# The last matrix product of a hybrid mLSTM and attention block: its buffers, its look-ahead, its sums and its weight pieces laid out anew

## The chip, the cores and the metric

The kernel runs on one core of a Trainium2 chip. The metric is the device time of one execution in microseconds (us), as the median of several runs. All arithmetic is on float32 data.

## The reference, cut to what matters

One block works on 1024 tokens with 16 meta tokens ahead of them, width 1024. The change lies in the end of it, and in the layout of four of its weights:

```python
mix = g_a * (y_a @ w_branch_a) + g_b * (y_b @ w_branch_b)
h = h + mix @ w_out
z = rms_norm(h, norm2_g) @ w_ff1
h = h + jnp.square(jax.nn.relu(z)) @ w_ff2
return h[:, N_META:]
```

`w_ff1` is 1024 x 4096 and `w_ff2` 4096 x 1024. In the kernel `w_branch_a` is `w_a`.

## The kernel before, in words

**Products.** A float32 operand is split into a high part (a copy in TensorE's fp32r type) and a low part (the operand minus its high part), and each product is three matmuls: high by high, low by high, high by low (`mm3`). The four large products named above also use a 2 x 2 block scheme with seven block products in place of eight (numbered 1 to 7); the price is sums of operand blocks beforehand and sums of results behind. A tile is 128 x 1024 float32 (4 KB per partition).

**The last stages, in the order of TensorE.** `cols_a` (four column pairs of `w_a`), `out_p` (`w_out`), `cols_1` (sixteen column pairs of `w_ff1`, w10 to w115; the squared relu of each goes to DRAM as `z2d`), and then `rows_2`, the last stage, which is `z2d` times `w_ff2`. `rows_2` is four groups f0 to f3 (`NG`), each a quarter of the inner dimension. A group has 14 products: seven block products in two halves, q = 0 and q = 1. In names, f1w16l is group 1, weight side, q = 1, block product 6, low part; z is the other side.

**What a group of the last stage does.** `quarters2` loads four z tiles (zr) and four weight tiles (w2r) for each q through SP's queue: 16 tiles a group. `parts` (class `Rows`, from L1240) splits them for products 1 and 2 as they are, then makes eight sums (s1, t1, and six in place) for each q, and splits their results for products 6, 7, 5, 4, 3. A split is a copy on ACT (`SC.copy` in `hilo`, L1086) and a subtraction (`rest`, L233) into two new tiles. So a group has 28 splits and 16 sums, of 128 x 1024 each. `mul` issues 24 matmuls of 512 columns for a product; behind the second half of a block product four PSUM banks (128 x 512 each, six banks in the pool `psx`) are added to that block product's accumulator (`out_2`, L1482): on ACT as plain copies for four of the seven in group 0, on DVE otherwise. In the last group `out_2` also adds accumulators to each other and sends 16 pieces to the output (L1510).

**Who does a sum.** `either` (L230) gives each sum and each remainder to DVE or to POOL, whichever by a kept account would be done first; the third argument makes POOL dearer. `share_gp` sets it (L1576): in the last stage it is `BULK` = 3.0.

**Order.** The list `seq` holds all products. Before product n is issued, `ensure(n + ah, n)` prepares products up to n + ah; `ah` is `AH2` = 2 in the last stage, so each product's splits and sums are written two products ahead. The loads of the next group's two halves are hooked 5 and 2 products ahead of its first (L1571). A scheduler orders each engine's instructions from this.

**Buffers.** Pool `slots` has 44 tiles (`NSLOT`, L27); loads, split parts and, in the last stage, all 14 accumulator tiles live there. Pool `late` has tag "r" with 7 tiles (`late`, L1072; s1 and t1 come from it) and tag "wr" with 3 for the pieces of `w_a` and `w_ff1` (`raw`, L1161).

**Weight pieces.** A piece of `w_a` and `w_ff1` is read as 128 x 8 x 128 out of the row-major matrix, 512 bytes at a time; a piece of `w_out` and `w_ff2` as 128 x 2 x 512, 2 KB at a time.

Of the kernel before, what the change touches and what calls it, by code (L numbers as in the profile page):

```python
# [17 lines left out]
S = 1024  # L18
# [21 lines left out]
KB, FF = 2, 9  # L40
D2 = 2
NP_ = 2
AH1, AH2, NE1, NE2, ZH, BULK = 5, 2, 1, 5, 11, 3.0
TCARGS = dict(schedule_with_timeline_sim=True)

C_G1, C_G2, C_CW, C_CB, C_NG, C_SK, C_GQ, C_GK, C_GB, NCOL = 0, 8, 16, 40, 48, 56, 64, 65, 66, 67
# [136 lines left out]
def build(tc, A, taps=None):  # L183
# [18 lines left out]
    def slot(name, dt=F32):  # L202
        return sp.tile([128, L], dt, name=name, tag="S")
# [949 lines left out]
    class Cols:  # L1153


        def __init__(self, name, src, z, out, raw_slot):
            self.name, self.src, self.z, self.out, self.raw_slot = name, src, z, out, raw_slot
            self.r, self.c, self.t = {}, {}, {}
            self.gen = self.parts()

        def raw(self, e):  # L1161
            if e not in self.r:
                n = f"{self.name}r{e}"
                t = slot(n) if self.raw_slot else LP.tile([128, 1024], F32, name=n, tag="wr", bufs=3)
                dma(t[:, 0:1024].rearrange("p (k c) -> p k c", k=8),
                    self.src[:, e * 128:e * 128 + 128].rearrange("(k p) c -> p k c", p=128))
                self.r[e] = t
            return self.r[e]

        def part(self, i, src):  # L1170
            c = late("c", F32R) if (self.name, i) in LATE_C else slot(f"{self.name}c{i}", F32R)
            SC.copy(c[:, 0:512], src)
            rest(c[:, 512:1024], src, c[:, 0:512], share_gp[0])
            self.c[i] = c
# [65 lines left out]
    class Rows:  # L1240


        def __init__(self, name, quarters, out):
            self.name, self.quarters, self.out = name, quarters, out
            self.q, self.z, self.w = {}, {}, {}
            self.gen = {}

# [1 line left out]
            if q not in self.q:  # L1249
                self.q[q] = self.quarters(q)  # L1250

        def part(self, q, i, a, b):
            self.z[q, i] = hilo(a, f"{self.name}z{q}{i}")
            self.w[q, i] = hilo(b, f"{self.name}w{q}{i}")

        def parts(self, q):
            self.load(q)
            c = slice(0, 1024)
            (a11, a12, a21, a22), (b11, b12, b21, b22) = [[t[:, c] for t in x] for x in self.q[q]]
            self.q[q] = None  # L1260
# [12 lines left out]
            sub(b21, b21, b11)
            for i, a, b in ((6, a11, b11), (7, a21, b12), (5, s1, t1), (4, a22, b21), (3, a12, b22)):
                self.part(q, i, a, b)
                yield

        def prep(self, i, q):
# [44 lines left out]
            V.scalar_tensor_tensor(g, b, 2.0, g, OP.mult, OP.add)  # L1323
        return out

    cols_a = [Cols(f"wa{p}", A["w_a"][:, p * 256:p * 256 + 256], za, out_a(p), False) for p in range(4)]
    sy = s_parts(yq, za, "y")
    NBS = ((0, 512), (512, 512))
    load_gb(0)
# [43 lines left out]
                SC.activation(o, pt, AF.Copy, scale=col(C_G2 + k))  # L1373

    def out_quarters(q):
        a = [ga[p, h_] for p, h_ in ((q, 0), (2 + q, 0), (q, 1), (2 + q, 1))]
        b = []
        for kh in range(2):
            for ch in range(2):
                t = slot(f"wo{q}{kh}{ch}")  # L1380
                r0 = kh * 512 + q * 256
                dma(t[:, 0:1024].rearrange("p (a c) -> p a c", a=2),
                    A["w_out"][r0:r0 + 256, ch * 512:ch * 512 + 512].rearrange("(a p) c -> p a c", p=128))
                b.append(t)
        return a, b

    def load_x2(t):
# [136 lines left out]
    def hook(d, n, fn):  # L1524
        d.setdefault(n, []).append(fn)
# [2 lines left out]
    n_o = len(seq)  # L1528
    seq += [(out_p, i, q) for i in (1, 2, 6, 5, 3, 7, 4) for q in range(2)]
    n_1 = len(seq)  # L1530
    group(cols_1, NE2)
    n_2 = len(seq)
    seq += [(o, i, q) for o in rows_2 for i in (1, 2, 6, 7, 5, 4, 3) for q in range(2)]

# [33 lines left out]
        hook(before, n - 7 if p >= NE2 else max(n - 5, n_1 + 2 * NE2), lambda p=p: (cols_1[p].raw(0), cols_1[p].raw(1)))  # L1568
    for g in range(1, NG):
        for q in range(2):  # L1570
            hook(before, n_2 + 14 * g - 5 + 3 * q, lambda g=g, q=q: rows_2[g].load(q))  # L1571

    for n, (o, i, q) in enumerate(seq):
        for fn in before.get(n, ()):
            fn()
        share_gp[0] = BULK if n >= n_1 + 2 * NE2 + 14 else 1.5 if n<n_o else 1.5 if n<n_1 else 1.0  # L1576
        ah = AH2 if n >= n_2 or n_o <= n < n_1 - 6 else AH1
        if n_1 <= n < n_1 + 2 * NE2:
            ah = n_1 + 2 * NE2 - 1 - n
        ensure(n + ah, n)  # L1580
        o.mul(i, q)
# [3 lines left out]
def layout(inp):  # L1585
# [16 lines left out]
    out["wk"] = f("mlstm_wk")
    out["mbias"] = f("na_meta_bias")
# [46 lines left out]
```

## Time and profile before

| | us |
|---|---|
| median of 3 runs | 1702.43 (1701.75 to 1706.6) |
| the profiled execution | 1708.2 |
| its span, first to last instruction | 1706.4 |
| TensorE (PE) busy | 1613.5 (95%) |
| VectorE (DVE) busy | 1237.2 (73%) |
| ScalarE (ACT) busy | 784.8 (46%) |
| GpSimd (POOL) busy | 525.9 (31%) |
| mean granted TensorE clock | 0.982 |
| last stage, from its first matmul to the end of the span | 1361.34 to 1706.40 |

The span is of one execution under the profiler, 5.8 us above the median of the plain runs in its own time; 1.8 us of that execution lie outside the span. Busy times are sums over an engine's instructions; matmuls are pipelined, so their recorded durations overlap, and the pace is read from their starts. The granted clock is a share of TensorE's full speed (1.00 is 2.4 GHz, 0.50 is 1.2 GHz).

### The profile page before, as it was taken

To read this page: it belongs to the slowest core of one execution; us is meant where nothing else is said; L and a number is where in the kernel's file an instruction comes from. 1 tells how busy PE (TensorE), PEld (TensorE's weight loads), DVE (VectorE), ACT (ScalarE), POOL (GpSimd) and SP (SyncE) were. 2 spreads that over 40 slices of the span, in tenths; PEclk is the share of its full clock that TensorE was granted. 3 is DMA by queue.
4 is the path that set the end of the run, shared out by engine and by line. 5 is a ranking of instruction groups with operands and counts; after the bars stand their busy time and mean duration, and the time that the engine had idled before them with its cause. 6 is when DMAs were issued, how large, how long until landed. Compare 5 with 4: busy or idle time off the path is not lost. (4 is left out here: it accounts for less than half of the span.)

```text
span 1706.4 us, 22334 instructions
## 1 busy us (share of the span) xinstructions
PE 1613.5 (95%) x8009; PEld 1361.6 (80%) x8009; DVE 1237.2 (73%) x2121; ACT 784.8 (46%) x1398; POOL 525.9 (31%) x509
## 2 busy tenths in 40 slices
PE   5999799999999999999899898899999989999998
PEld 4988789988989988888677676688888868777776
DVE  4438657574767686872689989786667787988897
ACT  6367666666747676752322444222222334333230
POOL 4110212122242222213567666610000042323274
PEclk9999999999999999999999899999999999999999
DMA  6352744546363443438547031143222735132311
GB/s 194 63 131 63 184 116 117 131 112 149 75 172 83 106 96 79 104 82 259 176 133 246 25 99 62 37 160 112 99 99 100 257 107 190 60 138 83 115 50 74
DMA packets 114190, 202.18 MB, mean 118 GB/s; under 512 B 10760, under 2 KB 62344, under 8 KB 114080
## 3 DMA queue, kind: packets, MB, share of 16 engines
q1 hardware_dynamic: 95648, 137.71, 24.3%
q0 software_dynamic: 18432, 63.05, 17.1%
q8 instruction: 63, 1.03, 0.2%
q14 instruction: 47, 0.39, 0.1%
HBM read 153.44 MB, written 38.76 MB: 113 GB/s over the span
## 5 line engine op out<-in xcount | busy, mean ns | idle before, releaser
L137 PE MATMUL g<-xh,wl 128*128 128x512 f32 (+3 forms) x832 | 304.2, 366 | 10.1 <-DMA wl<-w_in 10.1
L137 PE MATMUL g<-xh,wh 128*128 128x512 f32 (+3 forms) x832 | 306.2, 368 | 5.4 <-DVE xm L137 2.7
L137 PE MATMUL g<-xl,wh 128*128 128x512 f32 (+3 forms) x832 | 302.6, 364 | 0.0
L137 PEld LDWEIGHTS g<-xh,wl 128*128 128x128 f32 x832 | 158.1, 190 | 29.6 <-DMA wl<-w_in 11.5
L137 PEld LDWEIGHTS g<-xh,wh 128*128 128x128 f32 x832 | 158.5, 191 | 24.2 <-DVE xm L137 3.0
L137 PEld LDWEIGHTS g<-xl,wh 128*128 128x128 f32 x832 | 158.5, 190 | 16.8
L174 POOL DMA_DIRECT2D wl<-w_in x44 | 40.5, 922 | 166.5 <-ACT wl L137 74.6
L137 DVE TENSOR_TENSOR acc<-acc,pf 128x512 f32<-128x512 f32 x96 | 63.0, 677 | 9.8 <-PE pf L137 9.8
L137 DVE CUSTOM_DVE_ANT_0 P<-ps,bt 128x400 f32<-128x400 f32 x64 | 36.0, 570 | 45.4 <-PE pp L137 21.6
L137 ACT ACTIVATE wl<-wh 128x1024 fp32r<-128x1024 f32 (+1 forms) x52 | 51.5, 991 | 25.1 <-PE g L137 11.7
L137 ACT COPY pu<-pf 128x512 f32<-128x512 f32 x20 | 11.7, 585 | 108.1 <-PE pf L137 108.1
L137 DVE SCALAR_TENSOR_TENSOR C<-C,decb,pu 128x258 f32<-128x258 f32 x52 | 23.4, 480 | 33.9 <-PE pu L137 33.5
L137 ACT ACTIVATE P<-P,mn 128x400 f32<-128x400 f32 x64 | 40.3, 630 | 15.2 <-DVE mn L137 14.7
L137 DVE SCALAR_TENSOR_TENSOR zq<-zq 128x512 f32<-128x512 f32 x64 | 46.2, 721 | 0.7
L137 POOL COPY bt<-mbias 128x32 f32<-128x32 f32 x32 | 8.3, 262 | 115.7 <-DVE mn L137 115.6
L161 POOL DMA_DIRECT2D wh<-w_in x44 | 29.4, 668 | 37.4 <-ACT plo L137 10.2
L137 DVE TENSOR_TENSOR zq<-pf,pu 128x512 f32<-128x512 f32 x32 | 21.9, 686 | 24.9 <-PE pf L137 24.9
L137 DVE TENSOR_SCALAR P<-P,sm 128x384 f32<-128x384 f32 (+1 forms) x128 | 38.5, 364 | 0.9
L137 DVE TENSOR_TENSOR zq<-pf,sp 128x512 f32<-128x512 f32 x32 | 22.0, 687 | 23.6 <-PE pf L137 23.4
L137 DVE TENSOR_TENSOR ptl<-pp,pth 128x384 fp32r<-128x384 f32 x64 | 35.5, 555 | 2.7 <-ACT pth L137 2.0
L137 DVE TENSOR_TENSOR pu<-pf,pu 128x512 f32<-128x512 f32 x40 | 27.3, 683 | 12.9 <-PE pf L137 12.9
L137 ACT CAST pth<-pp 128x512 fp32r<-128x512 f32 x60 | 34.0, 581 | 5.4 <-PE pp L137 5.2
(2379 smaller groups left out, 5040.3 us busy)
## 6 DMA issues: line engine op xcount, KB each, us to landing
wh<-w_in POOLq DMA_DIRECT2D x44, 512.0 KB, 5.3
wl<-w_in POOLq DMA_DIRECT2D x44, 512.0 KB, 5.7
z2d<-zq SPq DMA_DIRECT2D x32, 512.0 KB, 4.4
zr<-z2d SPq DMA_DIRECT2D x32, 512.0 KB, 4.0
w2r<-w_ff SPq DMA_DIRECT2D x32, 512.0 KB, 8.3
bt<-rpbd SPq DMA_DIRECT2D x256, 32.0 KB, 2.6
xcl<-xc POOLq DMA_DIRECT2D x8, 520.0 KB, 5.5
ra<-rowd SPq DMA_DIRECT2D x8, 512.0 KB, 4.2
```

The lines of the kernel that those rows point to most:

```text
L137: return fn(out, *a, **k)
L161: self.nc.gpsimd.dma_start(h[:, 0:src.shape[-1]], src)
L174: self.nc.gpsimd.dma_start(l[:, 0:w], src, accum_op=OP.add)
```

## The change

On the host `w_a` and `w_ff1` are stored block by block (`blk`) and `w_out` and `w_ff2` quarter by quarter (`qtr`), so that each piece that a DMA reads is 4 KB in a row per partition. In the last stage:

- accumulators 1, 6, 7 and half of 5 lie in `late` tiles, 4 and the other half of 5 in the "wr" tiles, 2 and 3 in slots; s1 and t1 move from `late` to slots;
- products are prepared four ahead (`AH3`) and the next group's loads are hooked 7 and 4 products ahead; the first group's loads are hooked 10 and 5 ahead;
- `share_gp` is 1e6 from eight products before the stage: no sum or remainder goes to POOL;
- of the 14 splits of each q, three (the weight side of block products 2 and 3, the z side of 4, whose operands are tiles as loaded) make the low part another way: ACT writes the negated high part, and a DMA that POOL issues adds the operand to it from DRAM;
- the last two column pairs of `w_ff1` (w114, w115) alternate product by product, and w115's pieces lie in slots.

```diff
-AH1, AH2, NE1, NE2, ZH, BULK = 5, 2, 1, 5, 11, 3.0
+AH1, AH2, AH3, NE1, NE2, NT2, ZH, BULK = 5, 2, 4, 1, 5, 2, 11, 3.0
...
+    def raw_late(name):
+        return LP.tile([128, 1024], F32, name=name, tag="wr", bufs=3)
...
-                dma(t[:, 0:1024].rearrange("p (k c) -> p k c", k=8),
-                    self.src[:, e * 128:e * 128 + 128].rearrange("(k p) c -> p k c", p=128))
+                dma(t[:, 0:1024], self.src[e])
...
+        def split(self, t, src, name):
+            if src is None:
+                return hilo(t, name)
+
+            h_, l_ = slot(name + "h", F32R), slot(name + "l", F32R)
+            SC.copy(h_[:, 0:S], t)
+            SC.activation(l_[:, 0:S], h_[:, 0:S].bitcast(F32), AF.Copy, scale=-1.0)
+            nc.gpsimd.dma_start(l_[:, 0:S], src, accum_op=OP.add)
+            return h_, l_
...
-            self.part(q, 2, a12, b21)
+            self.part(q, 2, a12, b21, None, e21)
             yield
-            s1, t1 = late("s1")[:, c], late("t1")[:, c]
+            s1, t1 = self.tmp("s1")[:, c], self.tmp("t1")[:, c]
...
-            for i, a, b in ((6, a11, b11), (7, a21, b12), (5, s1, t1), (4, a22, b21), (3, a12, b22)):
-                self.part(q, i, a, b)
+            n = None
+            for i, a, b, da, db in ((6, a11, b11, n, n), (7, a21, b12, n, n), (5, s1, t1, n, n), (4, a22, b21, d22, n),
+                                    (3, a12, b22, n, e22)):
+                self.part(q, i, a, b, da, db)
...
-                    dma(t[:, 0:1024].rearrange("p (a c) -> p a c", a=2),
-                        A["w_ff2"][r0:r0 + 256, ch * 512:ch * 512 + 512].rearrange("(a p) c -> p a c", p=128))
-                    b.append(t)
+                    src = A["w_ff2"][2 * c + kh, ch]
+                    dma(t[:, 0:1024], src)
+                    b.append((t, src))
...
-                acc[i] = load_h2(f"acc{i}", i) if i in (2, 3, 4) else [slot(f"acc{i}{n}") for n in range(2)]
+                new = {2: (slot, slot), 3: (slot, slot), 4: (raw_late, raw_late), 5: (late, raw_late)}.get(i, (late, late))
+                acc[i] = [fn(f"acc{i}{n}") for n, fn in enumerate(new)]
...
-    rows_2 = [Rows(f"f{g}", quarters2(g), out_2(g)) for g in range(NG)]
+    rows_2 = [Rows(f"f{g}", quarters2(g), out_2(g), slot) for g in range(NG)]
...
-    group(cols_1, NE2)
+    group(cols_1[:-NT2], NE2)
+
+    seq += [(o, i, 0) for i in (1, 6, 2, 7, 5, 3, 4) for o in cols_1[-NT2:]]
...
-            hook(before, n_2 + 14 * g - 5 + 3 * q, lambda g=g, q=q: rows_2[g].load(q))
+            hook(before, n_2 + 14 * g - 7 + 3 * q, lambda g=g, q=q: rows_2[g].load(q))
+    for q in range(2):
+        hook(before, n_2 - 10 + 5 * q, lambda q=q: rows_2[0].load(q))
...
-        share_gp[0] = BULK if n >= n_1 + 2 * NE2 + 14 else 1.5 if n<n_o else 1.5 if n<n_1 else 1.0
-        ah = AH2 if n >= n_2 or n_o <= n < n_1 - 6 else AH1
+        share_gp[0] = 1e6 if n >= n_2 - 8 else BULK if n >= n_1 + 2 * NE2 + 14 else 1.5 if n < n_1 else 1.0
+        ah = AH3 if n >= n_2 else AH2 if n_o <= n < n_1 - 6 else AH1
```

**What stands on POOL at the start of the last stage.** Before, the last sum of column pair w115 and then sums and remainders of group f0:

```order
L137 TENSOR_TENSOR w115c_12751<-tt,w115c_12751 128x512
L137 TENSOR_TENSOR t_12990<-w2r_12871,w2r_12869 128x1024
L137 TENSOR_TENSOR w2r_12909<-w2r_12915,t_13110 128x1024
L137 TENSOR_TENSOR zr_12863<-zr_12863,zr_12861 128x1024
L137 TENSOR_TENSOR w2r_12873<-w2r_12873,w2r_12869 128x1024
L137 TENSOR_TENSOR f0z16l<-zr_12901,f0z16h 128x1024
L137 TENSOR_TENSOR f0z07l<-zr_12865,f0z07h 128x1024
```

And now the last sum before the stage, and behind it the six DMAs of group f0:

```order
L137 TENSOR_TENSOR tt<-w115r_12575,w115r_12573 128x512
L1265 DMA f0w02l<-w_ff 128x1024
L1265 DMA f0w12l<-w_ff 128x1024
L1265 DMA f0z04l<-z2d 128x1024
L1265 DMA f0z14l<-z2d 128x1024
L1265 DMA f0w03l<-w_ff 128x1024
L1265 DMA f0w13l<-w_ff 128x1024
```

The 50 elementwise instructions that POOL had in the last stage are gone; in their place POOL issues 24 DMAs there, six a group, and nothing else.

**DVE in group f0, up to the remainder f0w16l.** Before (zq and pu are results of the last column pair):

```order
L137 TENSOR_TENSOR f0z12l<-zr_12903,f0z12h 128x1024
L137 TENSOR_TENSOR w2r_12911<-w2r_12915,w2r_12911 128x1024
L137 TENSOR_TENSOR f0w12l<-w2r_12913,f0w12h 128x1024
L137 TENSOR_TENSOR f0z06l<-zr_12861,f0z06h 128x1024
L137 SCALAR_TENSOR_TENSOR zq_12961<-zq_12961 128x512
L137 TENSOR_TENSOR f0w06l<-w2r_12869,f0w06h 128x1024
L137 TENSOR_TENSOR zq_12898<-pf,pu 128x512
L137 SCALAR_TENSOR_TENSOR zq_12961<-zq_12961 128x512
L137 TENSOR_TENSOR zr_12903<-zr_12903,zr_12901 128x1024
L137 TENSOR_TENSOR f0w16l<-w2r_12909,f0w16h 128x1024
```

And now:

```order
L137 TENSOR_TENSOR f0z06l<-zr_12764,f0z06h 128x1024
L137 TENSOR_TENSOR f0w06l<-w2r_12772,f0w06h 128x1024
L137 TENSOR_TENSOR s_13053<-zr_12880,zr_12882 128x1024
L137 TENSOR_TENSOR t_13054<-w2r_12886,w2r_12884 128x1024
L137 TENSOR_TENSOR zr_12880<-zr_12876,zr_12880 128x1024
L137 TENSOR_TENSOR w2r_12884<-w2r_12890,t_13054 128x1024
L137 TENSOR_TENSOR w2r_12886<-w2r_12890,w2r_12886 128x1024
L137 TENSOR_TENSOR zr_12876<-s_13053,zr_12876 128x1024
L137 TENSOR_TENSOR w2r_12888<-w2r_12888,w2r_12884 128x1024
L137 TENSOR_TENSOR zr_12878<-zr_12878,zr_12876 128x1024
L137 TENSOR_TENSOR f0z16l<-zr_12876,f0z16h 128x1024
L137 TENSOR_TENSOR f0w16l<-w2r_12884,f0w16h 128x1024
```

All sums of both halves of f0 now stand on DVE ahead of f0z16l and f0w16l. Back from the twelve rows shown to the last evacuation of column pair w115 stand nine more instructions of 128x1024 and three of 128x512.

**DVE in group f1, up to the remainder f1w16l.** Before:

```order
L137 TENSOR_TENSOR acc_13075<-acc_13075,pf 128x512
L137 TENSOR_TENSOR w2r_13355<-w2r_13355,w2r_13351 128x1024
L137 TENSOR_TENSOR acc_13075<-acc_13075,pf 128x512
L137 TENSOR_TENSOR zr_13475<-zr_13475,zr_13473 128x1024
L137 TENSOR_TENSOR acc_13076<-acc_13076,pf 128x512
L137 TENSOR_TENSOR f1w12l<-w2r_13485,f1w12h 128x1024
L137 TENSOR_TENSOR acc_13076<-acc_13076,pf 128x512
L137 TENSOR_TENSOR f1z06l<-zr_13343,f1z06h 128x1024
L137 TENSOR_TENSOR w2r_13485<-w2r_13485,w2r_13481 128x1024
L137 TENSOR_TENSOR f1w16l<-w2r_13481,f1w16h 128x1024
```

And now:

```order
L137 TENSOR_TENSOR zr_13423<-zr_13419,zr_13423 128x1024
L137 TENSOR_TENSOR w2r_13427<-w2r_13433,t_13636 128x1024
L137 TENSOR_TENSOR w2r_13429<-w2r_13433,w2r_13429 128x1024
L137 TENSOR_TENSOR zr_13419<-s_13635,zr_13419 128x1024
L137 TENSOR_TENSOR acc_13169<-acc_13169,pf 128x512
L137 TENSOR_TENSOR w2r_13431<-w2r_13431,w2r_13427 128x1024
L137 TENSOR_TENSOR acc_13169<-acc_13169,pf 128x512
L137 TENSOR_TENSOR acc_13170<-acc_13170,pf 128x512
L137 TENSOR_TENSOR zr_13421<-zr_13421,zr_13419 128x1024
L137 TENSOR_TENSOR acc_13170<-acc_13170,pf 128x512
L137 TENSOR_TENSOR f1z16l<-zr_13419,f1z16h 128x1024
L137 TENSOR_TENSOR f1w16l<-w2r_13427,f1w16h 128x1024
```

The f1 sums of q = 1 stand in one run, with evacuations of f0's and f1's products between them. Of the whole chain behind f0's last product, 18 instructions of 128x1024 and 9 of 128x512 end with f1w16l; in f2 and f3 the sums start before the group does.

## Rows read from the trace of the kernel before

**Rows 1.** The profile page, part 1: busy us, share of the span, instructions.
```profile
PE 1613.5 (95%) x8009; PEld 1361.6 (80%) x8009; DVE 1237.2 (73%) x2121; ACT 784.8 (46%) x1398; POOL 525.9 (31%) x509
```

**Rows 2.** Windows: us, busy of PE, PEld, DVE, ACT, POOL, clock, DMA, GB/s.
```profile
1147.40:1341.87 194.47, 194.47 (x841) 157.70 (x840) 132.51 (x211) 43.75 (x79) 13.03 (x10) 1.00 0.36 121
1361.34:1445.66 84.32, 79.03 (x338) 62.78 (x336) 69.14 (x55) 35.91 (x45) 26.61 (x8) 1.00 0.43 150
1445.66:1527.84 82.18, 79.55 (x337) 64.05 (x336) 72.88 (x63) 27.79 (x29) 25.82 (x9) 0.98 0.29 103
1527.84:1610.50 82.66, 78.72 (x338) 62.79 (x336) 71.39 (x64) 27.90 (x29) 23.09 (x9) 1.00 0.29 102
1610.50:1702.44 91.94, 83.63 (x337) 65.55 (x335) 81.20 (x72) 22.90 (x23) 50.80 (x24) 0.94 0.14 52
1702.44:1706.40 3.96, 0.00 (x0) 0.00 (x0) 0.69 (x1) 0.00 (x0) 0.00 (x0) 1.00 0.35 132
```

**Rows 3.** Waits of 1361 to 1706: engine, waited for: us, times, longest us.
```profile
PEld pf L137 <- DVE acc L137: 23.0, 12, 3.4
...
PE pf L137 <- DVE acc L137: 17.8, 11, 2.9
```

**Rows 4.** Timeline of PE, f3: start us, us, instruction, idle before it.
```profile
1652.58 0.50 PE L137 MATMUL pf<-f3w07h,f3z07h 128*128 128x512 f32 x1 [2.13 <-DVE acc L137]
...
1653.69 0.63 PE L137 MATMUL pf<-f3w07h,f3z07h 128*128 128x512 f32 x1
1654.11 0.63 PE L137 MATMUL pf<-f3w07l,f3z07h 128*128 128x512 f32 x1
```

**Rows 5.** Windows of three stretches behind such waits, columns as above.
```profile
1453.50:1457.50 4.00, 3.49 (x10) 2.82 (x11) 4.00 (x6) 0.00 (x0) 0.00 (x0) 0.69 0.00 0
1652.50:1659.80 7.30, 6.50 (x15) 4.66 (x16) 6.83 (x6) 2.94 (x3) 7.30 (x5) 0.54 0.00 1
1669.80:1674.00 4.20, 3.93 (x10) 3.18 (x11) 3.62 (x4) 0.00 (x0) 3.91 (x2) 0.59 0.00 0
```

**Rows 6.** Timeline of DVE beside sums of POOL.
```profile
1370.98 3.44 DVE L137 TENSOR_TENSOR f0z12l<-zr,f0z12h 128x1024 fp32r<-128x1024 f32 x1
...
1377.69 3.40 DVE L137 TENSOR_TENSOR f0w12l<-w2r,f0w12h 128x1024 fp32r<-128x1024 f32 x1
```

**Rows 7.** Timeline of POOL, the same stretch.
```profile
1369.94 3.40 POOL L137 TENSOR_TENSOR zr<-zr,zr 128x1024 f32<-128x1024 f32 x1
...
1376.64 3.37 POOL L137 TENSOR_TENSOR f0z16l<-zr,f0z16h 128x1024 fp32r<-128x1024 f32 x1
```

**Rows 8.** Timeline of DVE behind that, POOL idle.
```profile
1386.69 0.68 DVE L137 SCALAR_TENSOR_TENSOR zq<-zq 128x512 f32<-128x512 f32 x1
1387.29 1.21 DVE L137 TENSOR_TENSOR zr<-zr,zr 128x1024 f32<-128x1024 f32 x1
1388.42 1.21 DVE L137 TENSOR_TENSOR f0w16l<-w2r,f0w16h 128x1024 fp32r<-128x1024 f32 x1
```

**Rows 9.** Groups of POOL in the last stage: busy us, mean ns, idle before.
```profile
L137 POOL TENSOR_TENSOR acc<-acc,acc 128x512 f32<-128x512 f32 x16 | 30.1, 1897 | 9.9 <-DVE acc L137 9.9
```

**Rows 10.** Tile wl: the copies into it, who waited for it, landing.
```profile
L137 ACT ACTIVATE wl<-wh x52: 622/1054/1092, 11.9 to 834.5; 128x1024 fp32r<-128x1024 f32 x44, 128x512 fp32r<-128x512 f32 x8
...
  PE g L137: 10.8, 6
...
DMA to landing us min/median/max: 3.9/5.8/15.8
```

**Rows 11.** The profile page, part 6: landing of DMAs, KB each, us.
```profile
zr<-z2d SPq DMA_DIRECT2D x32, 512.0 KB, 4.0
w2r<-w_ff SPq DMA_DIRECT2D x32, 512.0 KB, 8.3
```

**Rows 12.** Waits of PE in 840 to 1361.
```profile
PE g L137 <- DMA wl<-w_b: 0.6, 1, 0.6
```

**Rows 13.** Window with the first group's loads, columns as in rows 2.
```profile
1341.00:1361.00 20.00, 20.00 (x88) 16.21 (x87) 15.41 (x17) 5.67 (x7) 2.42 (x1) 1.00 0.91 338
```

More of the change, by code (lines that the diff above doesn't have):

```diff
@@ L1240, in build, with __init__ @@
     class Rows:
-        def __init__(self, name, quarters, out):
-            self.name, self.quarters, self.out = name, quarters, out
+        def __init__(self, name, quarters, out, tmp):
+            self.name, self.quarters, self.out, self.tmp = name, quarters, out, tmp
             self.q, self.z, self.w = {}, {}, {}
@@ L1250, in load, with part @@
                 self.q[q] = self.quarters(q)
-        def part(self, q, i, a, b):
-            self.z[q, i] = hilo(a, f"{self.name}z{q}{i}")
-            self.w[q, i] = hilo(b, f"{self.name}w{q}{i}")
+        def part(self, q, i, a, b, da=None, db=None):
+            self.z[q, i] = self.split(a, da, f"{self.name}z{q}{i}")
+            self.w[q, i] = self.split(b, db, f"{self.name}w{q}{i}")
+        def split(self, t, src, name):
[6 more added lines that the diff above has]
+            return h_, l_
         def parts(self, q):
@@ L1258, in parts @@
             c = slice(0, 1024)
-            (a11, a12, a21, a22), (b11, b12, b21, b22) = [[t[:, c] for t in x] for x in self.q[q]]
+            (a11, a12, a21, a22), (b11, b12, b21, b22) = [[t[:, c] for t, _ in x] for x in self.q[q]]
+            (_, _, _, d22), (_, _, e21, e22) = [[src for _, src in x] for x in self.q[q]]
             self.q[q] = None
@@ L1324, in out_a @@
         return out
-    cols_a = [Cols(f"wa{p}", A["w_a"][:, p * 256:p * 256 + 256], za, out_a(p), False) for p in range(4)]
+    cols_a = [Cols(f"wa{p}", A["w_a"][2 * p:2 * p + 2], za, out_a(p), False) for p in range(4)]
     sy = s_parts(yq, za, "y")
@@ L1375, in out_quarters @@
     def out_quarters(q):
-        a = [ga[p, h_] for p, h_ in ((q, 0), (2 + q, 0), (q, 1), (2 + q, 1))]
+        a = [(ga[p, h_], None) for p, h_ in ((q, 0), (2 + q, 0), (q, 1), (2 + q, 1))]
         b = []
@@ L1380, in out_quarters @@
                 t = slot(f"wo{q}{kh}{ch}")
-                r0 = kh * 512 + q * 256
-                dma(t[:, 0:1024].rearrange("p (a c) -> p a c", a=2),
-                    A["w_out"][r0:r0 + 256, ch * 512:ch * 512 + 512].rearrange("(a p) c -> p a c", p=128))
-                b.append(t)
+                dma(t[:, 0:1024], A["w_out"][kh * 2 + q, ch])
+                b.append((t, None))
         return a, b
@@ L1427, in finish_h @@
         norm2(t)
-    out_p = Rows("po", out_quarters, out_o)
+    out_p = Rows("po", out_quarters, out_o, late)
     z2d = dp.tile([16, 2, 128, 1024], F32, name="z2d")
@@ L1446, in out_1 @@
         return out
-    cols_1 = [Cols(f"w1{p}", A["w_ff1"][:, p * 256:p * 256 + 256], zz, out_1(p), p < 3) for p in range(16)]
+    cols_1 = [Cols(f"w1{p}", A["w_ff1"][2 * p:2 * p + 2], zz, out_1(p), p < 3 or p == 15) for p in range(16)]
     acc, HQ = {}, {2: (0, 0), 3: (0, 1), 4: (1, 0), 5: (1, 1)}
@@ L1458, in get @@
                     t = slot(f"zr{c}{kh}{h_}")
-                    dma(t[:, 0:1024], z2d[2 * c + kh, h_])
-                    a.append(t)
+                    src = z2d[2 * c + kh, h_]
+                    dma(t[:, 0:1024], src)
+                    a.append((t, src))
             for kh in range(2):
@@ L1463, in get, with load_h2 @@
                     t = slot(f"w2r{c}{kh}{ch}")
-                    r0 = (4 * c + 2 * kh) * 128
-                    dma(t[:, 0:1024].rearrange("p (a c) -> p a c", a=2),
-                        A["w_ff2"][r0:r0 + 256, ch * 512:ch * 512 + 512].rearrange("(a p) c -> p a c", p=128))
-                    b.append(t)
+                    src = A["w_ff2"][2 * c + kh, ch]
+                    dma(t[:, 0:1024], src)
+                    b.append((t, src))
             return a, b
         return get
-    def load_h2(name, i):
+    def load_h2(ts, i):
         h_, ch = HQ[i]
-        ts = []
-        for n in range(2):
-            t = slot(f"{name}{n}")
+        for n, t in enumerate(ts):
             r0 = h_ * 512 + n * 256
@@ L1478, in load_h2 @@
                 h2d[r0:r0 + 256, ch * 512:ch * 512 + 512].rearrange("(a p) c -> p a c", p=128))
-            ts.append(t)
         return ts
@@ L1484, in out @@
             if g == 0 and t == 0:
-                acc[i] = load_h2(f"acc{i}", i) if i in (2, 3, 4) else [slot(f"acc{i}{n}") for n in range(2)]
+                new = {2: (slot, slot), 3: (slot, slot), 4: (raw_late, raw_late), 5: (late, raw_late)}.get(i, (late, late))
+                acc[i] = [fn(f"acc{i}{n}") for n, fn in enumerate(new)]
+                if i in (2, 3, 4):
+                    load_h2(acc[i], i)
             if g == NG - 1 and i == 1 and t == 0:
-                acc["h"] = load_h2("hq", 5)
+                acc["h"] = load_h2([slot(f"hq{n}") for n in range(2)], 5)
             x = lambda j: acc[j][t // 2][:, lo(t % 2)]
@@ L1592, in layout @@
         w.reshape(w.shape[0] // 128, 128, -1, n).transpose(2, 1, 0, 3)).reshape(-1, 128, w.shape[0] // 128 * n)
+    qtr = lambda w: np.ascontiguousarray(
+        w.reshape(-1, 2, 128, 2, 512).transpose(0, 3, 2, 1, 4)).reshape(-1, 2, 128, 1024)
     w = f("w_in")
@@ L1595, in layout @@
     out["w_g"] = blk(w[:, 2048:2064], 16)[0]
-    out["w_a"] = f("w_branch_a")
+    out["w_a"] = blk(f("w_branch_a"), 128)
     out["w_b"] = blk(f("w_branch_b"), 128)
-    out["w_out"] = f("w_out")
-    out["w_ff1"] = f("w_ff1")
-    out["w_ff2"] = f("w_ff2")
+    out["w_out"] = qtr(f("w_out"))
+    out["w_ff1"] = blk(f("w_ff1"), 128)
+    out["w_ff2"] = qtr(f("w_ff2"))
     out["wq"] = f("mlstm_wq")
```

## The prediction

> **What bounds the kernel now.** First the page's busy line: PE has 95% of the span [rows 1], so the question is where its missing time lies and what the change can return of it. The pace of PE without a wait is read from a quiet stretch of `cols_1`: 841 matmuls in 194.47 us at clock 1.00 [rows 2], so 194.47 / 841 = 0.2312 us each, 5.55 us for a product of 24, 77.7 us for a group of 14 products, 310.7 us for four. The reader is to set that beside the four windows of the groups [rows 2]: 84.32, 82.18, 82.66 and 91.94 us, in sum 341.1. The last stage loses 6.6 + 4.5 + 5.0 + 14.2 = **30.4 us** (rounded at the end). Behind it stand 3.96 us of tail.
>
> Who keeps PE waiting there is in the list of waits: PE's weight loads and matmuls both name DVE's accumulator additions, 23.0 and 17.8 us [rows 3] (the two overlap). A matmul needs a PSUM bank, the bank needs its evacuation, and DVE is late with it. A wait has a second price: in f3, behind a gap of 2.13 us, matmuls start 0.42 us apart (1653.69, 1654.11) [rows 4], and three such stretches have a granted clock of 0.69, 0.54 and 0.59 [rows 5], between the levels of 1.2 and 2.4 GHz. Against full clock they lose 0.31 x 4.0 + 0.46 x 7.3 + 0.41 x 4.2 = 6.3 us, 2.1 each.
>
> Why DVE is late is in two timelines. A 128x1024 remainder on DVE takes 3.4 us [rows 6] beside POOL's sums, which take 3.4 us too [rows 7]; a moment later, with POOL idle, the same operation takes 1.21 us and starts 1.13 behind the one ahead, and a 128x512 one starts the next 0.60 later [rows 8]. So a sum handed to POOL saves DVE nothing: DVE stands for as long as POOL works.
>
> **The change part by part.**
> *No sums on POOL.* POOL had 50 elementwise instructions in the stage; their busy time is 26.61 + 25.82 + 23.09 + 50.80 = 126 us [rows 2]. DVE takes what the DMAs don't. Its work in a group is then 28 - 6 = 22 remainders and 16 sums, 38 x 1.135 = 43.1 us, and 28 evacuations x 0.60 = 16.8 us: 60 us, 77% of a group's 77.7 us. In f0, ACT takes 16 of the evacuations as before. In f3 the 32 additions between accumulators (16 of them on POOL before, at 1.9 us [rows 9]) come to 32 x 0.60 = 19 us; but no next group is prepared there, which takes off about as much. DVE is no longer the bound in the mean; what remains is its order.
>
> *Four products ahead, loads earlier.* An evacuation now stands behind preparation that is less urgent, and DVE is in order, so a run of sums could hold a bank up: the longest run in f0 is 21 instructions, 24 us. There it decides by the remainder f0w16l, the last thing that the sixth product needs. From the last evacuation of column pair w115 (its product ends at 1361.34 in the old trace; call this E), DVE does 21 instructions x 1.135 and 3 x 0.60 = 25.6 us, and starts some 0.5 later: E + 26.1. PE needs it after four products and half of the fifth, since its order alternates the halves: 4 x 5.55 + 2.8 = E + 25.0. That is about 1.1 us late, and if it brings one stretch at lower clock, 2.1 us more: 3 us. In f1 the chain behind f0's last product is 18 x 1.135 + 9 x 0.60 = 25.8 us, and PE needs the result after 18 matmuls more than the 22.2 us of four products: 26.4. Just in time. In f2 and f3 the sums start before the group, so some 5 us are spare. I take 3 us for the stage, bounds 0 and 16 (the latter the rival A).
>
> *Low parts by DMA.* 24 of them. Each takes one remainder (1.13 us) off DVE and puts a second copy on ACT, where a copy into a low part takes 1.05 us by tile wl [rows 10]: 6 more a group, 6 us beside 23 to 36 us that ACT is busy in a group [rows 2]. It hides there. The DMA itself must land before PE comes: landing takes 3.9 to 15.8 us, median 5.8 [rows 10], and four products of look-ahead are 22 us. So 0; the other end is rival B.
>
> *Accumulators elsewhere, s1 and t1 in slots.* Before, 14 accumulator tiles + 16 loaded + 12 split tiles (three products) = 42 of 44 slots. After: 4 + 16 + 4 (s1, t1) + 20 (five products of four tiles) = 44 of 44. This carries the look-ahead and costs nothing by itself, if a load finds its slot in time: rival C.
>
> *4 KB weight pieces.* The w2r tiles land in 8.3 us where zr of the same size lands in 4.0 [rows 11], so transfers get cheaper. But no weight's landing keeps PE: between 840 and 1361 us the only DMA it waits for is one of 0.6 us, and not for a weight of this change [rows 12]. The DMA engines are 0.43 busy or less in each group [rows 2], and 0.91 at the loads of f0 [rows 13], where PE runs on at 1.00. I take 0, with -1 to +3 us.
>
> *w114 and w115 in turn.* Same matmuls, same evacuations; PE is busy for 20.00 of 20.00 us there now [rows 13]. 0. All that comes before keeps its order. The tail has the same four evacuations and output DMA: 3.96 us as before.
>
> **The sum.** 30.4 - 3 = 27.4 us, against the profiled execution: its span 1706.4 becomes 1679.0. That execution was 1708.2 us, 5.8 above the median of the runs. If this excess is spread evenly, a fifth of it (341 of 1706 us) lies in the stage and is no loss of the median run: 1.2 us. So 26.2 off 1702.43: **1676 us**.
>
> **A rule against the change.** First the rows: the fills of tile wl are issued by POOL too, and PE waited 10.8 us for them, six times among 52 [rows 10]; so such fills can be late. The Trainium skill, page "SBUF — State Buffer", section "SBUF: two separate sides", says that a DMA issued from GpSimd has its descriptors written by GpSimd, and that some DVE operations lock it out of the ports while they run. By that rule the 24 fills would stand behind DVE, and with DVE 77% busy they would be late, as in rival B. The same page, section "Who interferes with whom", takes two-input sums of DVE (nearly all that DVE does here) out of it, but calls that inferred; the trace of before has no such DMA in this stage.
>
> **The rivals.**
> A. *DVE's order is too tight everywhere.* For: the chains of f0 and f1 come within about 1 us of the need, and durations under load may be longer than those of rows taken in one quiet moment. Against: f2 and f3 begin early. If each group loses 1.9 us and a stretch of low clock, 4 us, the loss is 16: 1702.4 - 14.4 = **1688 us**.
> B. *The DMA-made low parts come late.* For: the 10.8 us above. Against: they were prepared one weight ahead, here it is four products. 24/52 x 10.8 = 5.0 us, and a stretch of low clock of 2.1: 7 more than my sum, **1683 us**.
> C. *The slots are full, and loads wait for them: slower.* A group's 16 tiles of 0.524 MB take 24.8 us at 338 GB/s [rows 13]. With 44 of 44 taken a load may start only when split tiles of the group before come free. If a next group's first half (8 tiles) starts when the group itself does, each of three starts loses 12.4 us, 2.3 us of first splits (two at 1.13) and 2.1 of low clock: 17 us, 50 in all: 1676 + 50 = **1726 us**. It decides from 27.4 / 3 = 9.1 us lost per start. Against: the loads are hooked seven and four products ahead, 39 and 22 us, and the first half needs eight slots that the group before frees with its products.
> D. *The waits move but stay.* The waits for DVE could rest on the evacuations' place in its order rather than on POOL. Then nothing is gained, **1702 us**. Against: the same operation takes 2.8 times as long beside POOL [rows 6, 8].
>
> **How the numbers follow.** My forecast has 0.62, with a range of its own of 1671 (early stages give 3, no lateness) to 1682 (three times the lateness). A 0.16, B 0.10, C 0.07, D 0.05. The predicted time is the forecast's. Two in ten may stand outside: C and D and the upper part of A make 0.16, the lower end leaves a little, so 1669 to 1690. About 0.3%, 5 us, is what a measurement of this kernel can tell from no change: faster by more 0.88 (forecast, A, B), within 0.05 (D), slower 0.07 (C).
>
> **What would show it.** Right: DVE's 128x1024 operations in the stage all near 1.2 us; POOL with no busy time but 24 DMA issues; groups of about 80, 78, 78 and 78 us; nearly no wait of PE for accumulator additions; clock 1.00 in each group. A shows as waits of PE for DVE's remainders (names with 6l) at the starts of groups; B as waits for a DMA into w02l, z04l or w03l; C as waits of SP's queue for a tile's release, and PE waiting for copies of 01 parts. Wrong altogether: if DVE's remainders stay at 2 to 3 us with POOL idle, since then POOL was not the cause; or if the stretches before 1361 us change by more than 3 us.

## The result, and the profile after

The changed kernel takes 1677.88 us in the median of four runs (1677.13 to 1679.02), against 1704.29 us for the kernel before (four runs): a ratio of 0.9846, with an interval of 0.9827 to 0.9865, so 1.5% faster. Forecast were 1676 us. The profiled execution took 1679.02 us, with a span of 1677.2 us where 1679.0 were forecast.

Busy time by engine, part 1 of the profile page of the changed kernel, answers to [rows 1]:

```profile
PE 1602.5 (96%) x8009; PEld 1356.6 (81%) x8009; DVE 1188.2 (71%) x2149; ACT 807.6 (48%) x1422; POOL 416.6 (25%) x481
```

PE has 96% of a span that is 29 us shorter. The four groups of the last stage and the tail, as windows with the columns of [rows 2]:

```profile
1359.82:1439.47 79.65, 78.16 (x337) 63.03 (x336) 56.30 (x57) 41.75 (x50) 5.22 (x6) 1.00 0.67 208
1439.47:1517.40 77.93, 77.93 (x337) 63.11 (x336) 62.90 (x68) 33.70 (x34) 5.22 (x6) 1.00 0.51 149
1517.40:1595.29 77.89, 77.89 (x337) 63.10 (x336) 60.84 (x67) 33.93 (x34) 5.19 (x6) 1.00 0.50 149
1595.29:1673.25 77.96, 77.96 (x337) 62.90 (x335) 69.34 (x90) 23.49 (x24) 3.49 (x4) 1.00 0.32 88
1673.25:1677.20 3.95, 0.00 (x1) 0.00 (x0) 0.69 (x1) 0.00 (x0) 0.00 (x0) 0.79 0.35 133
```

The groups take 79.65, 77.93, 77.89 and 77.96 us, in sum 313.4, where 310.7 are the pace without a wait. The stage's loss of 30.4 us is down to 2.7. The granted clock is 1.00 in all four groups (it was 0.94 in the last). In place of POOL's 126 us of sums stand 19 us of DMA issues (22 of the 24; two came ahead of the stage). The stage also begins 1.5 us earlier, at 1359.82 instead of 1361.34; in the traces of e4 and e12 it begins at 1356.88 and 1361.33 us, and neither has another order of work ahead of the last two column pairs, so this much is scatter.

Of PE's waits for DVE's accumulator additions [rows 3] none is left. From 1100 us to the end the list of PE's waits has one row:

```profile
PE pf L137 <- DVE f0w16l L137: 1.5, 1, 1.5
```

DVE's timeline in f0 (start, duration) shows sums at full speed; beside POOL they took 3.4 us [rows 6]:

```profile
1369.66 1.21 DVE L137 TENSOR_TENSOR zr<-s,zr 128x1024 f32<-128x1024 f32 x1
1370.80 1.21 DVE L137 TENSOR_TENSOR w2r<-w2r,w2r 128x1024 f32<-128x1024 f32 x1
```

### The profile page after: what moved, and what is told of

It reads as the page before. It is cut to its first block, busy times and chain, and to the rows that moved or that the text cites. A ratio compares the mean times of both kernels' runs of the same rounds, so it can differ in the third digit from the quotient of the medians.

```text
span 1677.2 us, 22352 instructions
## 1 busy us (share of the span) xinstructions
PE 1602.5 (96%) x8009; PEld 1356.6 (81%) x8009; DVE 1188.2 (71%) x2149; ACT 807.6 (48%) x1422; POOL 416.6 (25%) x481
## 4 chain that ended last, share of the span: by engine, by line
PE 73%; DVE 11%; DMA 7%; issue 5%; ACT 3%; POOL 1%; SPq 0%; DVEq 0%; POOLq 0%; ACTq 0%
PE pf L137 36%; PE g L137 26%; DMA wl<-w_in 3%; DVE ga L137 2%; PE po L137 2%; PE pt L137 2%; PE pp L137 1%; PE ps L137 1%; PE pn L137 1%; DMA ra<-masks 1%; PE pi L137 1%; PE pu L137 1%; DMA gbd<-gbq 1%; DVE zq L137 1%; DVE gt L137 1%
```

## The experiments

All ratios are to the kernel before on the same chip; its medians there were 1706 to 1708 us. Two theories stood at the start: that DVE's time beside POOL's sums was the loss (theory 1), or the short look-ahead (theory 2).

**e1: the change, but sums go to POOL.**

```diff
-        share_gp[0] = 1e6 if n >= n_2 - 8 else BULK if n >= n_1 + 2 * NE2 + 14 else 1.5 if n < n_1 else 1.0
+        share_gp[0] = BULK if n >= n_1 + 2 * NE2 + 14 else 1.5 if n < n_1 else 1.0
```

> The changed kernel with one thing undone: POOL takes sums and remainders in the last stage again (share_gp 3.0). Theory 1 (DVE stands still while POOL works on SBUF tiles, and that was the loss): DVE's 128x1024 operations beside POOL's go back to about 3.4 us, PE waits for accumulator additions again, and most of the 26 us goes: 1693 to 1704 us. Theory 2 (two products of look-ahead were the loss, four are the cure): nothing of this matters, 1676 to 1682 us.

Measured: 1714.23 us, ratio 1.0036 (1.0020 to 1.0053). The whole gain is gone and a little more, outside what either theory said. Windows of its four groups, and two of PE's waits in the stage:

```profile
1359.02:1448.36 89.34, 80.58 (x338) 64.65 (x336) 59.65 (x50) 42.04 (x50) 28.93 (x14) 0.94 0.63 191
1448.36:1534.06 85.70, 80.04 (x337) 64.01 (x336) 69.23 (x59) 33.69 (x34) 37.14 (x16) 0.98 0.46 135
1534.06:1620.39 86.33, 79.78 (x338) 63.70 (x337) 67.25 (x58) 33.89 (x34) 34.85 (x16) 0.96 0.45 134
1620.39:1707.40 87.01, 80.95 (x337) 64.79 (x335) 77.10 (x69) 23.67 (x24) 52.06 (x26) 0.96 0.29 79
```

```profile
PE pf L137 <- DVE acc L137: 18.3, 8, 5.7
PE pf L137 <- ACT f0w16h L137: 7.4, 1, 7.4
```

Every group loses 8 to 12 us against 77.7, the clock is below 1.00 in each, and PE waits for accumulators again, and for f0w16h, a high part whose operand is a sum. Theory 2 falls: four products of look-ahead, the other buffers, the DMA-made low parts and the 4 KB pieces are all in this kernel. Why it is slower than the kernel before was not tried; in f0 it lost 5 us more than before did (89.34 against 84.32 [rows 2]).

**e2: the kernel before, but no sum to POOL in the last stage.**

```diff
-        share_gp[0] = BULK if n >= n_1 + 2 * NE2 + 14 else 1.5 if n<n_o else 1.5 if n<n_1 else 1.0
+        share_gp[0] = 1e6 if n >= n_2 - 8 else BULK if n >= n_1 + 2 * NE2 + 14 else 1.5 if n<n_o else 1.5 if n<n_1 else 1.0
```

> The kernel before with one thing done: no sum on POOL from eight products ahead of the last stage; accumulators, look-ahead of two, loads, pieces and low parts as before. DVE then has 28 remainders, 16 sums and 28 evacuations a group, 44 x 1.135 + 28 x 0.60 = 66.7 us of 77.7. Theory 1: most of the gain comes from this alone, 1680 to 1690 us, with PE's waits for accumulator additions below 8 us. Theory 2: the look-ahead is still two products, so about 1704 us.

Measured: 1677.67 us, ratio 0.9823 (0.9787 to 0.9858). One number in one line gives the whole gain, more than expected. Windows of its four groups:

```profile
1358.87:1437.22 78.35, 78.21 (x337) 63.02 (x336) 65.52 (x65) 35.67 (x45) 0.00 (x0) 1.00 0.46 162
1437.22:1515.05 77.83, 77.83 (x337) 63.08 (x336) 67.52 (x74) 27.78 (x29) 0.00 (x0) 1.00 0.31 109
1515.05:1592.92 77.87, 77.87 (x338) 63.11 (x336) 68.34 (x74) 28.09 (x29) 0.00 (x0) 1.00 0.31 108
1592.92:1670.85 77.93, 77.93 (x337) 62.93 (x335) 71.13 (x92) 22.90 (x23) 0.00 (x0) 1.00 0.17 61
```

78.35, 77.83, 77.87 and 77.93 us: a loss of 1.3 us in place of 30.4. PE's list of waits in the stage is empty. DVE does all 44 operations of 128x1024 of a group and is busy for 65 to 71 us, where it was busy for 69 to 81 us with POOL's help [rows 2]: with help it worked longer.

**e3: the change, but without the DMA-made low parts.**

```diff
-            if src is None:
-                return hilo(t, name)
+            return hilo(t, name)
```

> The changed kernel with the 24 low parts made by DVE subtractions instead of ACT and a DMA. DVE has 66.7 us of work a group in place of 60. Theory 1: two of the six come ahead of f0w16l, so that wait grows from 1.5 to 3.8 us, perhaps with a stretch at lower clock; f1 loses up to 2 us; f2 and f3 nothing: 1679 to 1685 us. Rival (the relief of DVE by the DMAs is the main part): over 1690 us.

Measured: 1682.81 us, ratio 0.9853 (0.9816 to 0.9890), as theory 1 said. Windows of f0 and f1, and PE's waits in the stage:

```profile
1360.84:1444.17 83.33, 79.84 (x337) 64.07 (x336) 67.89 (x66) 35.94 (x44) 0.00 (x0) 0.98 0.44 158
1444.17:1522.06 77.89, 77.89 (x337) 63.09 (x336) 67.40 (x73) 27.66 (x28) 0.00 (x0) 1.00 0.28 108
```

```profile
PE pf L137 <- DVE f0w16l L137: 1.8, 1, 1.8
PE pf L137 <- ACT f0w16h L137: 1.7, 1, 1.7
```

All of it lies in f0: 83.33 us, 5.6 over the pace, with waits for the high and the low part of the same operand and the clock at 0.98. f1 is at the pace with DVE at 67 us. So in this order of work the DMAs buy 3.7 us in f0 (79.65 against 83.33) and nothing later; the interval of the ratio reaches over that of the changed kernel, so the time alone would not show it. In the order of e2 they aren't needed.

**e4: the change with two products ahead.**

```diff
-AH1, AH2, AH3, NE1, NE2, NT2, ZH, BULK = 5, 2, 4, 1, 5, 2, 11, 3.0
+AH1, AH2, AH3, NE1, NE2, NT2, ZH, BULK = 5, 2, 2, 1, 5, 2, 11, 3.0
```

> The changed kernel with two products prepared ahead in place of four. Theory 1: DVE has the time, only its order gets tighter, and evacuations stand behind fewer sums: 1678 to 1688 us. Theory 2: most of the gain goes, 1695 to 1704 us.

Measured: 1676.21 us (1673.75 to 1681.05), ratio 0.9822 (0.9776 to 0.9867). No difference from four ahead that can be told; the wait for f0w16l is the same 1.5 us.

**e5: the kernel before with 4 KB weight pieces.** The host stores the four weights by `blk` and `qtr`, and the loads read them so:

```diff
-                dma(t[:, 0:1024].rearrange("p (k c) -> p k c", k=8),
-                    self.src[:, e * 128:e * 128 + 128].rearrange("(k p) c -> p k c", p=128))
+                dma(t[:, 0:1024], self.src[e])
```

> The kernel before with the weights' layout of the change alone: every piece 4 KB in a row. PE waits for no weight in the trace of before, so my theory says no change, 1701 to 1708 us beside before; the landing of the second product's weights goes from 8.3 us towards the 4.0 of z tiles of the same size. A rival, that cheaper transfers are a part of the gain, says 1690 to 1700 us.

Measured: 1705.55 us, ratio 0.9992 (0.9975 to 1.0009): nothing. The landing of w2r went from 8.3 us [rows 11] to 7.6 only, so its size was a miss: it isn't the pieces that make w2r slower than zr.

**e6: e2 with idle work on POOL.** For each weight-side high part of the summed products POOL subtracts it from itself into a tile that nobody reads:

```diff
+            if self.name[0] == "f" and i in (6, 7, 5, 4, 3):
+                h = self.w[q, i][0][:, 0:1024].bitcast(F32)
+                nc.gpsimd.tensor_sub(late("idle")[:, 0:1024], h, h)
```

> The kernel of e2 (no sum on POOL in the last stage, all else as before) with 40 subtractions added on POOL, ten a group, each of a high part from itself into a tile that nobody reads: POOL reads 128x1024 tiles for some 40 x 3.4 = 136 us (126 us of POOL's work there before), and no engine waits for a result of it. Theory 1a (DVE stands still while POOL reads tiles): DVE's sums and remainders beside them take about 3.4 us again, PE waits for DVE, and the time goes to 1690 to 1712 us. Theory 1b (the loss was that somebody waited for POOL's slow results): 1675 to 1681 us as e2.

Measured: 1704.31 us, ratio 0.9984 (0.9970 to 0.9998). The added work is not used by anyone, and it costs 26.6 of the 29 us that e2 had gained. So nobody had to wait for a result of POOL; POOL's running was enough (theory 1a). Only the tiles that POOL reads come free later: ACT's first copies in f2 and f3 waited 5.8 and 6.4 us for that. In e12 below the same two waits are 6.9 and 7.4 us and the kernel is some 21 us faster, so they are not what cost. Windows of its four groups:

```profile
1356.81:1436.49 79.68, 78.15 (x338) 63.01 (x337) 74.43 (x61) 35.96 (x45) 30.02 (x10) 1.00 0.46 159
1436.49:1520.03 83.54, 79.86 (x338) 64.12 (x337) 82.39 (x78) 27.97 (x29) 24.50 (x10) 0.98 0.28 101
1520.03:1602.13 82.10, 79.08 (x337) 62.75 (x336) 79.04 (x73) 27.87 (x29) 26.88 (x10) 1.00 0.30 103
1602.13:1692.35 90.22, 81.53 (x337) 64.97 (x335) 87.13 (x91) 22.67 (x23) 24.23 (x10) 0.94 0.11 39
```

DVE has the same work as in e2 and is busy for 74 to 87 us with it, not for 65 to 71. Most of the loss lies behind f0 (2.0, 5.8, 4.4 and 12.5 us). Timelines of DVE and of POOL in the same stretch of f0, and a subtraction of POOL in f1 that began while DVE was at an evacuation:

```profile
1387.76 2.91 DVE L137 TENSOR_TENSOR f0z17l<-zr,f0z17h 128x1024 fp32r<-128x1024 f32 x1
1390.60 1.27 DVE L137 TENSOR_TENSOR acc<-acc,pf 128x512 f32<-128x512 f32 x2
...
1393.43 2.91 DVE L137 TENSOR_TENSOR f0z05l<-s,f0z05h 128x1024 fp32r<-128x1024 f32 x1
```

```profile
1386.72 2.87 POOL L1257 TENSOR_TENSOR idle<-f0w07h 128x1024 f32<-128x1024 f32 x1
1389.56 2.87 POOL L1257 TENSOR_TENSOR idle<-f0w17h 128x1024 f32<-128x1024 f32 x1
...
1448.82 1.90 POOL L1257 TENSOR_TENSOR idle<-f1w06h 128x1024 f32<-128x1024 f32 x1 [26.96 <-ACT f1w06h L137]
```

A subtraction of POOL takes 2.87 us between DVE's remainders and 1.90 where nothing holds it up; DVE's remainder takes 2.91 beside it and 1.21 alone [rows 8]. So each takes nearly the time of both. The 3.4 us of POOL's sums in [rows 7] hold such waiting too: the shortest of that size in the stage took 2.4 us. But the two evacuations at 1390.60 take 1.27 us together: they read one operand from PSUM. Over the whole stage, DVE's group of evacuations in this kernel is as fast as ever (677 ns before):

```profile
L137 DVE TENSOR_TENSOR acc<-acc,pf 128x512 f32<-128x512 f32 x96 | 63.1, 676 | 1.5 <-PE pf L137 1.4
```

PE's longest waits in it are for remainders at the head of a group (2.5 us are left for accumulator additions):

```profile
PE pf L137 <- DVE f3w16l L137: 6.5, 1, 6.5
PE pf L137 <- DVE f1w16l L137: 3.7, 1, 3.7
```

**e12: e2 with copies on POOL.** As e6, with `tensor_copy(late("idle")[:, 0:1024], h)`: one tile read instead of two.

> As e6, with 40 copies on POOL (one tile read, one written) in place of the 40 subtractions (two reads, one written). If DVE stands still for as long as POOL reads a tile, whatever it does with it, a remainder beside a copy takes as long as the copy, and the loss is e6's 26.6 us in the measure of POOL's busy time: with copies of 1 to 1.5 us, 1683 to 1695 us. If only POOL's work with two tiles holds DVE up: 1675 to 1681 us, remainders at 1.2 us.

Measured: 1683.45 us (1676.78 to 1686.51), ratio 0.9846 (0.9816 to 0.9876). 5.8 us over e2, at the low end of what was expected; on the medians alone, since the interval reaches to e2's. The timelines say more. POOL in f0:

```profile
1385.23 4.49 POOL L1257 COPY idle<-f0w16h 128x1024 f32<-128x1024 f32 x1 [18.51 <-ACT f0w16h L137]
1389.67 1.04 POOL L1257 COPY idle<-f0w07h 128x1024 f32<-128x1024 f32 x1
```

DVE there, and further on:

```profile
1385.33 1.22 DVE L137 TENSOR_TENSOR f0z16l<-zr,f0z16h 128x1024 fp32r<-128x1024 f32 x1
1386.46 1.22 DVE L137 TENSOR_TENSOR f0w16l<-w2r,f0w16h 128x1024 fp32r<-128x1024 f32 x1
1387.60 1.22 DVE L137 TENSOR_TENSOR f0z07l<-zr,f0z07h 128x1024 fp32r<-128x1024 f32 x1
1388.73 1.28 DVE L137 TENSOR_TENSOR acc<-acc,pf 128x512 f32<-128x512 f32 x2
...
1399.13 2.06 DVE L137 TENSOR_TENSOR f0z15l<-s,f0z15h 128x1024 fp32r<-128x1024 f32 x1
```

and POOL further on:

```profile
1398.54 1.57 POOL L1257 COPY idle<-f0w15h 128x1024 f32<-128x1024 f32 x1 [1.54 <-ACT f0w15h L137]
```

A copy that nothing holds up takes 1.04 us. The first one took 4.49: it began at 1385.23, while DVE did remainders one behind the other, and ended at 1389.72, within DVE's two evacuations from PSUM (1388.73 to 1390.01). The one at 1398.54 overlaps DVE's remainder of 1399.13, which takes 2.06 us instead of 1.21. So each engine waits for the other, and not always in turn: the first copy stood behind three remainders. One tile that POOL reads is enough, with one that it writes; the runs do not tell these two apart. The Trainium skill, page "SBUF — State Buffer", section "Who interferes with whom", has the rule for this: a DVE operation with two operands in SBUF and a GpSimd operation that reads SBUF exclude each other for a whole instruction, and a DVE operation with at most one SBUF operand, outside DVE's two-port modes, goes free. The traces agree, with 2.91 against 1.21 us and with the evacuations' 676 ns.

**e8: block product 5 third in f0.** In the changed kernel, for f0 alone, the order is 1, 2, 5, 6, 7, 4, 3:

```diff
             sub(t1, b12, b11)
+            early5 = self.name == "f0"
+            if early5:
+                self.part(q, 5, s1, t1)
+                yield
```

> The changed kernel with another order in group f0 alone: block product 5, which needs only s1 and t1, comes third, ahead of 6 and 7. The one wait left in the stage (1.5 us for f0w16l, 2 us in f0 beside the pace) should go, since f0w15l stands some eleven instructions earlier than f0w16l did and f0w16l is needed 11 us later: f0 at 77.8 us, 1.5 to 2 us less than the changed kernel, 1674 to 1678 us. If the wait only moves to another remainder of f0, 1677 to 1680 us.

Measured: 1675.71 us (1674.58 to 1677.39), ratio 0.9822 (0.9807 to 0.9836). PE's list of waits from 1100 us on is empty, so the wait for f0w16l is gone and no other took its place. The 2.2 us in the medians are about as large as was expected (1.5 to 2), but the intervals overlap, so the time alone would not show it.

**e9: e2 with POOL out from `out_p` on. e10: out everywhere.** e9 sets `share_gp` to 1e6 from product `n_o`; e10 deletes the line `gp_helps[0] = True`, after which no sum or remainder goes to POOL at all.

> The kernel of e2 with POOL taken off sums and remainders from out_p on, not only in the last stage. Out_p and the start of cols_1 lose some 19 and 18 us beside PE's pace, with POOL busy for 69 and 34 us there and DVE for 104 and 47. Theory 1a: a sum handed to POOL saves DVE nothing there either, so DVE gets faster by up to (3.4 - 1.2) a sum, and 4 to 15 us go: 1662 to 1674 us. If DVE has no time to spare there (rival): no change or slower, 1676 to 1690 us.

> The kernel before with POOL never given a sum or remainder (cols_a too, where e9 left it 31 instructions and 54 us of work). PE loses next to nothing against its pace in cols_a, so theory 1a expects little beyond e9: 1654 to 1659 us; if DVE has no time for it there, 1660 to 1668.

Measured: e9 1656.98 us, ratio 0.9713 (0.9698 to 0.9727); e10 1651.24 us, ratio 0.9668 (0.9644 to 0.9691). e9 gained 5 us more than expected; e10 came below its range. Two stretches, as windows (the first ends where `cols_a` begins, the second runs from `out_p` to the last column pair that still lost time): before, e9 and e10.

```profile
780.00:849.63 69.63, 63.93 (x258) 49.55 (x258) 33.52 (x33) 21.01 (x27) 31.27 (x23) 0.95 0.73 227
928.55:1147.38 218.83, 195.44 (x821) 153.85 (x820) 195.84 (x192) 83.31 (x118) 124.75 (x71) 0.95 0.23 79
```

```profile
780.00:848.25 68.25, 62.42 (x253) 48.37 (x251) 32.24 (x32) 21.14 (x27) 31.97 (x23) 0.95 0.72 228
927.10:1127.90 200.80, 189.25 (x821) 150.82 (x820) 179.00 (x240) 85.53 (x123) 8.43 (x16) 0.97 0.25 87
```

```profile
780.00:842.23 62.23, 59.59 (x252) 46.60 (x251) 33.85 (x38) 20.02 (x26) 10.29 (x14) 1.00 0.80 249
921.11:1121.14 200.03, 188.82 (x821) 151.11 (x820) 177.91 (x239) 85.85 (x123) 8.37 (x16) 0.97 0.25 86
```

The second stretch has the same 821 matmuls. It took 218.83 us and takes 200.80 and 200.03: 18 us from e9's step, with DVE's busy time down from 196 to 179 us though it has 48 operations more. The first stretch has the 6 us of e10, with the clock at 1.00 instead of 0.95. So the expectation of e10 looked in the wrong place: `cols_a` had no time to give, but the splits and sums ahead of it did; there PE waited 5.1 us for DVE's gate tiles and waits 1.0 now.

**e11: the changed kernel with e8 and e10 on top.**

> The changed kernel with block product 5 third in f0 (as e8) and POOL never given a sum or remainder (as e10). If the rest of the change (accumulators elsewhere, four products ahead, low parts by DMA, 4 KB pieces) is worth nothing once POOL is out, this equals e10 within 3 us, 1653 to 1659 us; if it relieves DVE where DVE is scarce, 1645 to 1652 us.

Measured: 1649.06 us (1646.51 to 1651.40), ratio 0.9660 (0.9638 to 0.9682). The lowest time, but not to be told from e10, which is the kernel before less one line; so no worth of the rest of the change shows here.

## Why the prediction was right, point by point

- **The loss.** That 30.4 us of the stage were to be had, and that DVE's pace beside POOL was the reason, both stand: e2 returns 29.1 of them, and e6 takes nearly as much back with idle work (26.6 us in the medians).
- **The sum.** Forecast were 3 us of loss left; measured 2.7, of which f0 has 1.95 and the three others 0.2 each. That the sum came so close is in part luck: of the two terms in it one was too small and the other measured nothing (next point), and 1.2 us, f0's 0.5 beyond its wait and 0.7 in groups with no wait at all, were in no term. In the medians the gain was forecast as 26.2 us and measured as 26.4 (1704.29 less 1677.88). The 1.2 us taken off for the excess of the profiled execution are smaller than the scatter of the runs: no run shows them.
- **f0w16l.** It was forecast 1.1 us late and 2.1 us for a stretch at lower clock behind it. It was 1.49 us late, and the clock did not fall. Two rows of DVE, the last evacuation of w115 and f0w16l, and PE's timeline there (columns as in [rows 4]):

```profile
1361.05 0.68 DVE L137 TENSOR_TENSOR zq<-pf,sp 128x512 f32<-128x512 f32 x1
1385.56 1.22 DVE L137 TENSOR_TENSOR f0w16l<-w2r,f0w16h 128x1024 fp32r<-128x1024 f32 x1
```

```profile
1384.71 0.63 PE L137 MATMUL pf<-f0w16h,f0z16h 128*128 128x512 f32 x2
1386.83 0.50 PE L137 MATMUL pf<-f0w16l,f0z16h 128*128 128x512 f32 x1 [1.49 <-DVE f0w16l L137]
1387.16 0.39 PE L137 MATMUL pf<-f0w16h,f0z16l 128*128 128x512 f32 x1
1387.40 0.39 PE L137 MATMUL pf<-f0w16h,f0z16h 128*128 128x512 f32 x1
```

The row of 1384.71 stands for two matmuls. Behind the gap of 1.49 us the first start is 0.33 from the next, and from then on they are 0.23 to 0.24 apart, not 0.42 as in [rows 4]. So the term of 2.1 us was mis-sized: it measured nothing. The rows of before could have warned: PE waited 1.80 us for f0w12l in f0, and the clock of that window is 1.00 [rows 2]. The wait itself was 0.4 longer than worked out. E is 1359.82 here. DVE's chain was sized rightly, but began 1.2 us behind E where 0.5 were taken, and so ended at E + 27.0 instead of E + 26.1; PE came to need it at E + 25.5 instead of E + 25.0.
- **The DVE account.** 60 us of work a group was forecast; 56.30, 62.90, 60.84 and 69.34 were measured. But the prediction carried four products of look-ahead and the DMAs along as parts that cost nothing, and did not ask whether they were needed: e2 and e4 show that they weren't (without the DMAs, but with the rest of the change, f0 loses 3.7 us more: e3). For DVE, 67 of 77.7 us was little enough.
- **4 KB pieces.** Forecast 0, measured 0.9992 (e5). The reason given beside it, that transfers get cheaper, showed only as 7.6 us of landing in place of 8.3 (e5). In the changed kernel w2r lands later than before. The transfers of the last stage by tile (KB, us to landing):

```profile
w2r<-w_ff SPq DMA_DIRECT2D x24, 512.0 KB, 14.1
...
f1w13l<-w_ff POOLq DMA_DIRECT2D x1, 512.0 KB, 11.3
...
f3w03l<-w_ff POOLq DMA_DIRECT2D x1, 512.0 KB, 5.3
```

For the same 24 tiles e3, without the DMAs of POOL, has 6.6 us, and e4, with these DMAs but two products ahead, 7.8. All three have the 4 KB pieces, so the 14.1 us come with the DMAs and the longer look-ahead together, not from the pieces. No engine on the path waited for it.
- **Rival A** (1688 us) fell: f1, f2 and f3 have no wait of PE. **Rival B** (1683 us) fell: the 24 DMAs landed in 5.3 to 11.3 us, and no wait of PE for one is in the list. What the Trainium skill says in its page "SBUF — State Buffer", section "SBUF: two separate sides", of DMAs issued from GpSimd that starve while DVE runs in a two-port mode did not show beside DVE's sums of two SBUF operands; this agrees with the exception that its other section infers. **Rival C** (1726 us) fell, although SP's queue did wait for tiles, up to 37.8 us at one load: no wait of PE for a copy of a loaded tile is in the list, so the loads were hooked early enough. **Rival D** fell with e2.

## What to carry to other kernels

Before a sum is given to a second engine, compare the first engine's durations with and without it: a helper that takes 2.4 to 3.4 us for a sum of 1.2 us and holds the first engine up meanwhile was a loss here, though both look busy. A balance by kept accounts (`either`) can't see this, since its cost of an operation doesn't depend on what runs beside it. And when a change does five things, try each by itself: here one line, in the last stage alone, gave the whole gain (29 us, e2), and POOL out everywhere gave nearly twice as much (55 us, e10).

## What was not expected of the hardware

- DVE's two-operand work on SBUF tiles and POOL's work that reads a tile hold each other up: 2.91 us for DVE's remainder beside a subtraction of POOL, 2.06 beside a copy, 1.21 alone; and for POOL 2.87 us for a subtraction between DVE's remainders, 1.90 where nothing holds it up. The turns are not fair: a copy of 1.04 us took 4.49 behind three remainders.
- DVE's additions with one operand in PSUM are untouched by it: 677 ns in the kernel before, 680 after, 676 with idle work on POOL.
- A wait of 1.49 us of PE in f0 left the granted clock at 1.00, while one of 2.13 us in the kernel before was followed by matmuls 0.42 us apart. But one of 1.80 us in f0 of the kernel before left it at 1.00, and in e3 two of 1.72 and 1.78 us close together were followed by 3.4 us at 0.51. Whether the length of a wait alone decides is not shown.
